# A two-layer streaming encoder on one core: the second queries' scores in two halves, side by side in the values' banks

## The chip, the cores and the metric

The kernel runs on one core of one Trainium2 chip. The engines that appear below are PE (TensorE, the matmuls, with its weight loads shown as PEld), DVE (VectorE), ACT (ScalarE), POOL (GpSimd) and SP (SyncE, which here only issues DMAs). The metric is the device time of one execution in microseconds. The three runs of the kernel before took 1877.65 to 1878.27 us, with a median of 1878.14 us.

## The reference: what is computed

One sequence of 256 positions and width 2048 goes through two layers. Cut to what matters here, a layer is:

```python
h = rmsnorm(x, norm_g)
proj = h @ w_in                       # 2048 x 11328, cut into nine parts
u = c_a * sigmoid(c_glu)
u = depthwise_causal_conv(u, width=31) + conv_b
y_conv = (silu(layernorm(u)) * silu(c_gate)) @ w_proj_conv
q  = rmsnorm(q_down) @ w_uq           # 16 heads, 128 plain + 64 rotary
kv = rmsnorm(kv_down) @ w_ukv         # 16 heads, 128 key + 128 value
s  = q . k / sqrt(192), masked by chunks of 64, in query blocks of 128
o  = softmax(s) @ v
y_mla = (o * silu(m_gate)) @ w_proj_mla
x = x + (sigmoid(g_conv) * y_conv + sigmoid(g_mla) * y_mla) @ w_out
```

All of it is in fp32.

## The kernel before

**Parts.** The matmuls take fp32r operands. To keep fp32 accuracy every operand is split in two, a high part (its value rounded to fp32r) and a low part (what is left), and three products are added: high by high, low by high, high by low. Weights arrive in pieces of two k-tiles (`raw`, 512 KB). ACT makes the high part (`split_hi`, L191: a copy, the rows `hi<-raw`), and DVE the low part (`split_lo`, L211: a subtraction, the rows `lo<-raw,hi`). The pool has four buffers for high parts (L195) and three for low parts (`split`, L140).

**Slots.** A block of a product has 512 columns (384 or 320 in a few), and for each piece of weights it issues twelve matmuls (`order_of_products`, L278): two query tiles, two k-tiles, three products. These twelve matmuls are a slot. `product` (L292) issues ahead of the matmuls of slot i the high parts of the pieces up to i+3 and the low parts up to i+2. After the matmuls it calls `background` (L243), where everything else of the slot is issued.

**The planner.** `at_slot` notes a step with the slot in which it is due and its estimated cost on DVE and ACT. `background` gives each engine a budget for the slot (the matmuls' time less its share of the splitting, L245-247), runs the steps that are due and books their costs, and then runs entries of the queue `fill` as long as the DVE budget is above zero (L256-260). An entry may also wait for a mark, and the entries of `apply` wait for ACT's budget too (`scalar`, L258). With what is left of ACT's budget `assist` makes taps of the convolution on ACT. At the end of the slot `finish_late` (L266) runs what was put in `late`. Engines execute in the order of issue: the class `InOrder` (L118) ties each instruction to the one before it.

**What is in `fill`.** The depthwise convolution: 31 taps for each of eight blocks of 256 channels (`conv`, L869), on DVE, either as two multiply-adds or as one addition of a tap that ACT has scaled. Behind them stands the LayerNorm (`layernorm`, L919): the sums over channels by two small matmuls (`mu`, `var`), the inverse root on DVE, `apply` (L987, DVE) with its `silu` on ACT a slot later (`soon`), the turned gates (`turned_gate`, DVE transposes), `gated` (L1109, DVE) and `separated` (L1117), which splits the result into the high and low parts of `ycT`, on ACT and DVE. Two of the sixteen channel tiles of `ycT` come from each block; four tiles are a group c, which `gated` and `separated` handle as one.

**Who needs it.** The product `pconv` multiplies with `ycT`. Its first block runs in eight slots, and group c is first used in the slots 2c and 2c+1. `before_pconv` (L1176) stands ahead of the matmuls of each of these slots: where group c has not been issued, it runs `fill` without regard to budgets until it has, and issues the parts.

**Attention.** The pairs of heads are staged twelve slots apart (`attention`, L681; due slots in L66-67). Scores are due 17 slots after the pair's `ukv` product, the exponentials at 19, the turned probabilities' split at 29, the values at 32, the outputs at 34. So the scores of a pair fall into the same slot as `split_p` of the pair before, and three slots ahead of that pair's values. `scores` (L750) writes the first 128 queries' scores into the PSUM tile `s0` with the keys' high and low parts in two halves, and the last 128 queries' scores (against 256 keys) into `s1`, five matmuls of 256 columns a head that accumulate in one place. `maxima` (L774) adds the halves of `s0`, masks, and takes the maxima on DVE; `exponentials` (L788) reads `s1` from PSUM. PSUM has eight banks: four for the products, two for the tile `tp` (the values' output `o_ps`, and `mu` and `var`), one each for `s0` and `s1`.

**In two other places** a low part is made close to its high part: `ukv_evac` (L666) puts the subtraction of the values' low part into `late` of the same slot, and `split_p` (L807) does so with the probabilities'. `scale_k` (L694) makes ACT's scaling of the keys and DVE's rotary part in turn, tile by tile. `glu_evac` (L853) puts the product of the gated unit (`product_out`) into `late`.

Of the kernel before, what the change touches and what calls it, by code (L numbers as in the profile page):

```python
# [15 lines left out]
ALU = mybir.AluOpType  # L16
# [98 lines left out]
def trunk(ctx: ExitStack, tc: tile.TileContext, xT, x, g_in, pos, win, wuq, wukv, wpc, wpm, wo, cst, rows, invf, out):  # L115
# [102 lines left out]

    steps, clock, late = [], [0], []
    fill, budget, marks, owed, assist = deque(), {"vec": 0.0, "act": 0.0}, {}, [], []

    def at_slot(ahead, f, vec=0.0, act=0.0, first=False):
# [18 lines left out]
    def background(n):  # L243
        clock[0] += 1
        slot = 12 * (n / 2400 + 0.0133) - 0.04  # L245
        for e, split_us in (("vec", KS * n / 960 + 0.06), ("act", KS * n / 1066 + 0.04)):
            budget[e] = min(budget[e], 0.0) + slot - split_us
        while True:
            due = [e for e in steps if e[0] <= clock[0]]
            if not due:  # L250
                break
            steps[:] = [e for e in steps if e[0] > clock[0]]
            for _, costs, f in due:
                spend(costs)
                f()
        while fill and budget["vec"] > 0:  # L256
            after, slots, scalar = fill[0][1]
            if after and clock[0] < marks.get(after, 1 << 30) + slots or scalar and budget["act"] < 0:  # L258
                break
            run_fill()  # L260

        while assist and budget["act"] > 0.8 and assist[0]():
            budget["act"] -= 0.85
        finish_late()
# [132 lines left out]
    def rms_factor(out_ap, sums, n):  # L397
        ms = small.tile(list(sums.shape), F32, tag=f"ms{sums.shape[-1]}", name="ms")
        vec.tensor_scalar(ms, sums, 1.0 / n, EPS, op0=ALU.mult, op1=ALU.add)
        rsqrt(out_ap, ms)  # L400


    zeros = work.tile([P, 256], F32R, tag="junk", name="zeros")
# [122 lines left out]
    for l in range(DEPTH):  # L526
# [24 lines left out]
            act.activation(down[:, t, at : at + n], ps, AF.Copy, scale=rinv_x[:, t : t + 1])  # L551

        def down_after(down=down, qkc=qkc, ss_d=ss_d, r_d=r_d, kpe=kpe, ccq=ccq, ssq_t=ssq_t, gqk=gqk, row=row, C=C, ss_base=ss_base):
            ka = work.tile([P, T, ROPE], F32, tag="qa", name="ka")
            kb = work.tile([P, T, ROPE], F32, tag="qb", name="kb")
            kp = down[:, :, 2 * LORA :]

            def squares(t):
# [95 lines left out]
        def rotate_q(b, pair_of=pair_of, ccq=ccq, ssq_t=ssq_t):  # L654
            p = pair_of(b)
            both = lambda a: a.rearrange("p t (a c) -> p (t a) c", a=2).unsqueeze(2).broadcast_to([P, 2 * T, 2, HALF])
            qa = work.tile([P, T, 2, 2, HALF], F32, tag="qa", name="qa")
            qb = work.tile([P, T, 2, 2, HALF], F32, tag="qb", name="qb")
            qr = p["qr"].rearrange("p t a h c -> p (t a) h c")
            vec.tensor_mul(qa.rearrange("p t a h c -> p (t a) h c"), qr, both(ccq))  # L660
            vec.tensor_mul(qb.rearrange("p t a h c -> p (t a) h c"), qr, both(ssq_t))
            out = p["qk"][:, :, :, 4, :].rearrange("p t (h a) c -> p t h a c", h=2)
            vec.tensor_sub(out[:, :, :, 0, :], qa[:, :, 0], qb[:, :, 1])
            vec.tensor_add(out[:, :, :, 1, :], qb[:, :, 0], qa[:, :, 1])

        def ukv_evac(b, t, ps, pair_of=pair_of):  # L666

            p = pair_of(b)
            k = ps[:, : 2 * NOPE].rearrange("p (j h c) -> p j h c", j=4, h=2)
            v = ps[:, 2 * NOPE :].rearrange("p (h d) -> p h d", h=2)  # L670
            act.copy(p["vh"][:, t], v)
            act.copy(p["qk"][:, t, :, 2:4, :], k)
            late.append(lambda: vec.tensor_sub(p["vl"][:, t], v, p["vh"][:, t].bitcast(F32)))
            for h in range(2):
                junk = work.tile([P, 512], F32, tag="junk", name="junk")
                act.activation(
                    junk[:, :NOPE].rearrange("p (j c) -> p j c", c=32), k[:, :, h, :],
                    AF.Square, accum_out=p["ss"][:, 1, t, h : h + 1],
                )

        def attention(b, pair_of=pair_of, ss_d=ss_d, kpe=kpe, ccq=ccq, ssq_t=ssq_t, gqk=gqk, A=A):  # L681
# [11 lines left out]

            def scale_k():  # L694
                for t in range(T):
                    rk = st["r"][:, 1, t, :]
                    for h in range(2):
                        k = qk[:, t, :, 2 + h, :]
                        act.activation(k, k, AF.Copy, scale=rk[:, h : h + 1])
                    vec.tensor_mul(  # L700
                        qk[:, t, :, 5, :].rearrange("p (h a) c -> p h a c", h=2),
                        kpe[:, t].rearrange("p (a c) -> p a c", a=2).unsqueeze(1).broadcast_to([P, 2, 2, HALF]),
                        rk.unsqueeze(2).unsqueeze(3).broadcast_to([P, 2, 2, HALF]),
                    )
                out("qk", rows)

# [42 lines left out]

            def scores():  # L750
                s0 = s_p.tile([P, 2, 2, P], F32, tag="s0", name="s0")
                s1 = s_p.tile([P, 2, SEQ], F32, tag="s1", name="s1")

                for h in range(2):
                    qs = slice(0, P)
                    pe.matmul(s0[:, h], rope_t[:, 0, h, qs], rope_k[:, :, h, qs], start=True, stop=False)
                    pe.matmul(s0[:, h, 0, :], nope_t[:, 1, h, qs], nope_t[:, 2, h, qs], start=False, stop=False)
                    pe.matmul(s0[:, h], nope_t[:, 0, h, qs], nope_t[:, 2:4, h, qs], start=False, stop=True)
                for h in range(2):
                    qs = slice(P, SEQ)  # L760
                    terms = [
                        (rope_t[:, 0, h, qs], rope_t[:, 1, h, :]),
                        (nope_t[:, 0, h, qs], nope_t[:, 2, h, :]),
                        (nope_t[:, 0, h, qs], nope_t[:, 3, h, :]),
                        (nope_t[:, 1, h, qs], nope_t[:, 2, h, :]),
                        (rope_t[:, 0, h, qs], rope_l[:, h, :]),
                    ]
                    for n, (qa, ka) in enumerate(terms):
                        pe.matmul(s1[:, h, :], qa, ka, start=n == 0, stop=n == len(terms) - 1)
                st["s"] = s0, s1  # L770

                late.append(maxima)

            def maxima():  # L774
                s0, s1 = st["s"]
                sx = work.tile([P, 2, P], F32, tag="sx", name="sx")
                act.copy(sx, s0[:, :, 1, :])
                vec.tensor_add(sx, s0[:, :, 0, :], sx)
                for s, nkeys in ((sx, P), (s1, SEQ)):

                    vec.memset(s[:CHUNK, :, nkeys - CHUNK :], MASKED)
                nb = small.tile([P, T, 2], F32, tag="nb", name="nb")
                vec.tensor_reduce(nb[:, 0], sx, axis=AX.X, op=ALU.max, negate=True)
                vec.tensor_reduce(nb[:, 1], s1, axis=AX.X, op=ALU.max, negate=True)
                vec.tensor_mul(nb, nb, st["rs"])
                st["s"], st["nb"] = (sx, s1), nb

            def exponentials():  # L788

# [17 lines left out]
            def split_p():  # L807
                z = st["pr"].rearrange("p (b i s) -> p i b s", i=6, s=32)
                hi, lo = (A.pt[:, i].rearrange("p h (x b s) -> p (h x) b s", x=3, s=32) for i in range(2))

                def parts():
                    act.copy(hi, z)
                    vec.tensor_sub(lo, z, hi.bitcast(F32))

                late.append(parts)

            def values():

# [3 lines left out]
                for h in range(2):  # L822
                    o = st["o"][:, h]
                    pe.matmul(o, v[0][:, 0, h, :], pt[:, :, h, :SEQ], start=True, stop=False)
                    pe.matmul(o[:, 0, :], v[1][:, 0, h, :], pt[:, 0, h, :SEQ], start=False, stop=False)
                    pe.matmul(o[:, :, P:], v[0][:, 1, h, :], pt[:, :, h, SEQ:], start=False, stop=False)
                    pe.matmul(o[:, 0, P:], v[1][:, 1, h, :], pt[:, 0, h, SEQ:], start=False, stop=True)

            def outputs():
                o = A.o_sb[:, 2 * b : 2 * b + 2, :]  # L830
# [7 lines left out]
            at_slot(QK_TURN_AT, blockwise, 1.85)  # L838
            at_slot(NOPE_AT, split_nope, 0.0, 1.8)
            at_slot(ROPE_AT, split_rope, 0.0, 2.5)  # L840
            at_slot(SCORES_AT, scores, 1.85, 0.35)
            at_slot(EXP_AT, exponentials, 0.0, 3.3)
            at_slot(P_BACK_AT, lambda: back_in("p"))
            at_slot(P_TURN_AT, turn_p, 0.9)
            at_slot(P_SPLIT_AT, split_p, 0.9, 0.8)
            at_slot(VALUES_AT, values)
            at_slot(O_AT, outputs, 0.62, 0.6)

# [4 lines left out]
        def glu_evac(b, t, ps, us=us):  # L853
# [10 lines left out]
                vec.scalar_tensor_tensor(u, ps[:, :256], r, sg, op0=ALU.mult, op1=ALU.mult)  # L864
                turn(u, 256, lambda z: conv(b) if t == T - 1 else None, us[b][:, :, at : at + P], (0.4, 0.0))

            late.append(product_out)

        def conv(b, us=us, vs=vs, s1=s1, C=C):  # L869
            scaled = {}  # L870
# [314 lines left out]
        for kind, i, pl in planned:  # L1185
# [25 lines left out]
                product(pl, of_down(0), lambda t, ps, i=i: uq_evac(i, t, ps), costs=(0.0, 2.3))  # L1211
                at_slot(EVAC_AT + 1, lambda i=i: rotate_q(i), 1.2)
            elif kind == "ukv":
                product(pl, of_down(4), lambda t, ps, i=i: ukv_evac(i, t, ps), costs=(0.75, 2.6))
                attention(i)
                if i == NPAIR - 1:
                    layernorm()
# [125 lines left out]
```

## Time and profile before

| | |
|---|---|
| median of three runs | 1878.14 us (1877.65 to 1878.27) |
| profiled execution, own time | 1877.59 us |
| its span in the trace | 1875.8 us |
| PE busy | 1870.9 us, 8665 matmuls |
| PEld (weight loads) busy | 1583.1 us |
| DVE busy | 1577.6 us, 2419 instructions |
| ACT busy | 1369.1 us, 2482 instructions |
| POOL busy | 484.5 us |
| granted TensorE clock, mean | 1.0 |
| HBM | 236 GB/s over the span |

Busy times are those of the profile's first part. A matmul's row lasts until its result is out, and the rows of matmuls overlap, so PE's busy time is no measure of how close it is to its peak; the pace is read from when they start. Groups of instructions are named out<-in by the program's tiles; "x16" is a count, and the time after an arrow in brackets is idle time of the engine before the group and what ended it. Nearly all instructions stand under one line (L126, a helper that records them), so rows are told apart by tiles.

### The profile page before, as it was taken

The numbers are of one execution on the slowest core, as the hardware profiler recorded it, in microseconds if no ns is written. First come the engines' busy times: TensorE is split into PE (matmuls) and PEld (weight loads), VectorE is DVE, ScalarE is ACT, GpSimd is POOL, SyncE is SP. The second block draws the span as 40 slices with busy tenths as digits, with TensorE's granted clock in tenths as the row PEclk, the third lists the DMA queues.
The fourth block names the chain that finished last, engine by engine and source line by source line (L and its number), as shares of the span: only waits on it lengthen the run. The fifth ranks groups of instructions, "written<-read, shape, count | busy, mean of one in ns | idle before, by whom it ended". The sixth has DMA issues, their size and how long they took to land.

```text
span 1875.8 us, 27389 instructions
## 1 busy us (share of the span) xinstructions
PE 1870.9 (100%) x8665; PEld 1583.1 (84%) x8665; DVE 1577.6 (84%) x2419; ACT 1369.1 (73%) x2482; POOL 484.5 (26%) x942
## 2 busy tenths in 40 slices
PE   9999999999999999999999999999999999999999
PEld 8988888888888888888899888888888888888887
DVE  6899988889999988766679898888999999785664
ACT  7678888888888866644557688888899888574442
POOL 1055555432200000122221555555322000001210
PEclk9999999999999999999999999999999999999999
DMA  9677878777755566578876787786777555556774
GB/s 322 228 255 253 279 243 281 254 248 235 245 197 192 198 206 222 209 236 282 285 235 216 248 275 256 255 283 240 255 235 243 197 191 203 207 206 222 238 251 164
DMA packets 140113, 445.06 MB, mean 237 GB/s; under 512 B 23808, under 2 KB 29440, under 8 KB 139968
## 3 DMA queue, kind: packets, MB, share of 16 engines
q1 hardware_dynamic: 106272, 359.89, 55.7%
q0 software_dynamic: 32832, 82.62, 13.5%
q8 instruction: 68, 1.11, 0.2%
q10 hardware_dynamic: 864, 0.80, 0.1%
q14 instruction: 77, 0.63, 0.1%
HBM read 399.18 MB, written 44.04 MB: 236 GB/s over the span
## 4 chain that ended last, share of the span: by engine, by line
PE 100%; DVE 0%; DVEq 0%; issue 0%
PE acc L126 97%; PE s L126 2%; PE o_ps L126 1%; PE warm L126 0%; PE var L126 0%; PE mu L126 0%; DVE xres L126 0%; DVEq L1339 0%; DVE zeros L126 0%
## 5 line engine op out<-in xcount | busy, mean ns | idle before, releaser
L126 ACT CAST hi<-raw 128x1024 fp32r<-128x1024 f32 (+3 forms) x690 | 700.5, 1020 | 400.4 <-PE acc L126 349.0
L126 DVE TENSOR_TENSOR lo<-raw,hi 128x1024 fp32r<-128x1024 f32 (+3 forms) x690 | 814.1, 1183 | 193.6 <-PE acc L126 144.3
L126 PE MATMUL acc<-hi,hT 128*128 128x512 f32 (+2 forms) x1728 | 419.7, 382 | 0.0
L126 PEld LDWEIGHTS acc<-hi,hT 128*128 128x128 f32 x1728 | 319.6, 188 | 59.2
L126 ACT ACTIVATE tap<-u_t,cst 128x256 f32<-128x256 f32 x602 | 260.2, 497 | 3.2 <-DVE v_t L126 3.2
L126 PE MATMUL acc<-hi,h_hi 128*128 128x512 f32 (+2 forms) x864 | 260.8, 383 | 0.0
L126 PE MATMUL acc<-hi,h_lo 128*128 128x512 f32 (+2 forms) x864 | 260.1, 382 | 0.0
L126 PE MATMUL acc<-lo,h_hi 128*128 128x512 f32 (+2 forms) x864 | 229.6, 382 | 0.0
L126 PE MATMUL acc<-lo,hT 128*128 128x512 f32 (+2 forms) x864 | 229.3, 382 | 0.0
L126 DVE TENSOR_TENSOR v_t<-v_t,tap 128x512 f32<-128x512 f32 x301 | 207.0, 688 | 10.9 <-DVE v_t L126 0.5
L126 POOL DMA_DIRECT2D turned<-turn_d x88 | 49.1, 558 | 545.1 <-DVE v_t L126 315.8
L126 PEld LDWEIGHTS acc<-hi,h_lo 128*128 128x128 f32 x864 | 161.2, 188 | 30.2
L126 PEld LDWEIGHTS acc<-lo,h_hi 128*128 128x128 f32 x864 | 160.6, 188 | 30.0
L126 PEld LDWEIGHTS acc<-lo,hT 128*128 128x128 f32 x864 | 160.6, 188 | 29.9
L126 PEld LDWEIGHTS acc<-hi,h_hi 128*128 128x128 f32 x864 | 160.2, 188 | 29.1 <-ACT hi L126 0.2
L126 POOL DMA_DIRECT2D turn_d<-gate x184 | 100.1, 551 | 324.0 <-DVE gate L126 177.5
L126 DVE SCALAR_TENSOR_TENSOR v_t<-u_t,cst,v_t 128x256 f32<-128x256 f32 x358 | 153.8, 480 | 2.1
L126 PE MATMUL acc<-hi,ycT 128*128 128x512 f32 x512 | 127.8, 389 | 0.0
L126 PE MATMUL acc<-hi,yT 128*128 128x512 f32 x512 | 127.8, 389 | 0.0
L126 PE MATMUL acc<-hi,oT 128*128 128x512 f32 x512 | 127.7, 389 | 0.0
L126 PE MATMUL acc<-hi,qkc 128*128 128x512 f32 (+1 forms) x512 | 119.2, 364 | 0.0
L126 PEld LDWEIGHTS acc<-hi,ycT 128*128 128x128 f32 x512 | 96.1, 188 | 20.0
(169 smaller groups left out, 2209.9 us busy)
## 6 DMA issues: line engine op xcount, KB each, us to landing
raw<-in_win SPq DMA_DIRECT2D x382, 512.0 KB, 4.3
raw<-in_wpm SPq DMA_DIRECT2D x64, 512.0 KB, 3.2
raw<-in_wpc SPq DMA_DIRECT2D x64, 512.0 KB, 4.3
raw<-in_wo SPq DMA_DIRECT2D x64, 512.0 KB, 5.0
raw<-in_wukv SPq DMA_DIRECT2D x32, 512.0 KB, 3.6
turned<-turn_d POOLq DMA_DIRECT2D x56, 256.0 KB, 4.7
raw<-in_win SPq DMA_DIRECT2D x32, 384.0 KB, 4.7
raw<-in_wuq SPq DMA_DIRECT2D x32, 384.0 KB, 3.2
```

The lines of the kernel that those rows point to most:

```text
L126: ins = getattr(self.engine, name)(*a, **k)
```

## The change

The scores of the last 128 queries are no longer accumulated in one place. Their tile `s1` is now a tile of the pool `tp` (two banks, shared in turn with `o_ps`, `mu` and `var`), with the keys' high and low parts in two halves, as `s0` has them. Three matmuls a head, of 512, 256 and 512 columns, take the place of five of 256. `maxima` copies the second half of each to SBUF with ACT, adds the first half with DVE, and masks and reduces in SBUF. The sum of the second queries shares a buffer (`qab`) with the rotary products, which are now one tile in place of two. The exponentials read SBUF.

Beside this, other places are put in another order. The values' low part and the probabilities' low part are subtracted a slot after the high part (`at_slot(1, ...)`), with costs of their own. `scale_k` leaves the keys' rotary part and the DMAs behind it to `late`. The product of the gated unit goes into a new list, `early`, which runs ahead of `fill`. In `values` the second and the fourth matmul of a head change places. The planner's cost of the scores goes from (1.85, 0.35) to (2.5, 0.85), and 0.75 on `ukv` and 0.9 on `split_p` become 0.36 twice and 0.85 on the deferred steps.

```diff
             for _, costs, f in due:
                 spend(costs)
                 f()
+            while early:
+                early.pop(0)()
...
-            late.append(lambda: vec.tensor_sub(p["vl"][:, t], v, p["vh"][:, t].bitcast(F32)))
+            at_slot(1, lambda: vec.tensor_sub(p["vl"][:, t], v, p["vh"][:, t].bitcast(F32)), 0.36)
...
             def scale_k():
                 for t in range(T):
-                    rk = st["r"][:, 1, t, :]
                     for h in range(2):
                         k = qk[:, t, :, 2 + h, :]
-                        act.activation(k, k, AF.Copy, scale=rk[:, h : h + 1])
+                        act.activation(k, k, AF.Copy, scale=st["r"][:, 1, t, h : h + 1])
+                late.append(scale_rotary)
+
+            def scale_rotary():
+                for t in range(T):
                     vec.tensor_mul(
...
-                s1 = s_p.tile([P, 2, SEQ], F32, tag="s1", name="s1")
+                s1 = tp_p.tile([P, 2, 2, SEQ], F32, tag="tp", name="s1")
...
-                    terms = [
-                        (rope_t[:, 0, h, qs], rope_t[:, 1, h, :]),
-                        (nope_t[:, 0, h, qs], nope_t[:, 2, h, :]),
-                        (nope_t[:, 0, h, qs], nope_t[:, 3, h, :]),
-                        (nope_t[:, 1, h, qs], nope_t[:, 2, h, :]),
-                        (rope_t[:, 0, h, qs], rope_l[:, h, :]),
-                    ]
-                    for n, (qa, ka) in enumerate(terms):
-                        pe.matmul(s1[:, h, :], qa, ka, start=n == 0, stop=n == len(terms) - 1)
+                    pe.matmul(s1[:, h], rope_t[:, 0, h, qs], rope_k[:, :, h, :], start=True, stop=False)
+                    pe.matmul(s1[:, h, 0, :], nope_t[:, 1, h, qs], nope_t[:, 2, h, :], start=False, stop=False)
+                    pe.matmul(s1[:, h], nope_t[:, 0, h, qs], nope_t[:, 2:4, h, :], start=False, stop=True)
...
             def maxima():
-                s0, s1 = st["s"]
-                sx = work.tile([P, 2, P], F32, tag="sx", name="sx")
-                act.copy(sx, s0[:, :, 1, :])
-                vec.tensor_add(sx, s0[:, :, 0, :], sx)
-                for s, nkeys in ((sx, P), (s1, SEQ)):
+                sums = []
+                for s, nkeys, tag in zip(st["s"], (P, SEQ), ("sx", "qab")):
+                    sums.append(work.tile([P, 2, nkeys], F32, tag=tag, name="sx"))
+                    act.copy(sums[-1], s[:, :, 1, :])
+                for s, sx in zip(st["s"], sums):
+                    vec.tensor_add(sx, s[:, :, 0, :], sx)
+                for s, nkeys in zip(sums, (P, SEQ)):
                     vec.memset(s[:CHUNK, :, nkeys - CHUNK :], MASKED)
...
-                def parts():
-                    act.copy(hi, z)
-                    vec.tensor_sub(lo, z, hi.bitcast(F32))
-
-                late.append(parts)
+                late.append(lambda: act.copy(hi, z))
+                at_slot(1, lambda: vec.tensor_sub(lo, z, hi.bitcast(F32)), 0.85)
...
-                    pe.matmul(o[:, 0, :], v[1][:, 0, h, :], pt[:, 0, h, :SEQ], start=False, stop=False)
+                    pe.matmul(o[:, 0, P:], v[1][:, 1, h, :], pt[:, 0, h, SEQ:], start=False, stop=False)
                     pe.matmul(o[:, :, P:], v[0][:, 1, h, :], pt[:, :, h, SEQ:], start=False, stop=False)
-                    pe.matmul(o[:, 0, P:], v[1][:, 1, h, :], pt[:, 0, h, SEQ:], start=False, stop=True)
+                    pe.matmul(o[:, 0, :], v[1][:, 0, h, :], pt[:, 0, h, :SEQ], start=False, stop=True)
...
-            at_slot(SCORES_AT, scores, 1.85, 0.35)
+            at_slot(SCORES_AT, scores, 2.5, 0.85)
...
-            at_slot(P_SPLIT_AT, split_p, 0.9, 0.8)
+            at_slot(P_SPLIT_AT, split_p, 0.0, 0.8)
...
-            late.append(product_out)
+            early.append(product_out)
...
-                product(pl, of_down(4), lambda t, ps, i=i: ukv_evac(i, t, ps), costs=(0.75, 2.6))
+                product(pl, of_down(4), lambda t, ps, i=i: ukv_evac(i, t, ps), costs=(0.0, 2.6))
```

More of the change, by code (lines that the diff above doesn't have):

```diff
@@ L216, in split_lo @@
         done[i] = highs[i], lo, k.stop
-    steps, clock, late = [], [0], []
+    steps, clock, late, early = [], [0], [], []
     fill, budget, marks, owed, assist = deque(), {"vec": 0.0, "act": 0.0}, {}, [], []
@@ L400, in rms_factor, with rotary_tile @@
         rsqrt(out_ap, ms)
+    def rotary_tile():
+        qab = work.tile([P, 2, T, 2, ROPE], F32, tag="qab", name="qab")
+        return qab[:, 0], qab[:, 1]
     zeros = work.tile([P, 256], F32R, tag="junk", name="zeros")
@@ L553, in down_after @@
         def down_after(down=down, qkc=qkc, ss_d=ss_d, r_d=r_d, kpe=kpe, ccq=ccq, ssq_t=ssq_t, gqk=gqk, row=row, C=C, ss_base=ss_base):
-            ka = work.tile([P, T, ROPE], F32, tag="qa", name="ka")
-            kb = work.tile([P, T, ROPE], F32, tag="qb", name="kb")
+            ka, kb = (a[:, :, 0, :] for a in rotary_tile())
             kp = down[:, :, 2 * LORA :]
@@ L656, in rotate_q @@
             both = lambda a: a.rearrange("p t (a c) -> p (t a) c", a=2).unsqueeze(2).broadcast_to([P, 2 * T, 2, HALF])
-            qa = work.tile([P, T, 2, 2, HALF], F32, tag="qa", name="qa")
-            qb = work.tile([P, T, 2, 2, HALF], F32, tag="qb", name="qb")
+            qa, qb = (a.rearrange("p t a (h c) -> p t a h c", h=2) for a in rotary_tile())
             qr = p["qr"].rearrange("p t a h c -> p (t a) h c")
@@ L702, in scale_k @@
                         kpe[:, t].rearrange("p (a c) -> p a c", a=2).unsqueeze(1).broadcast_to([P, 2, 2, HALF]),
-                        rk.unsqueeze(2).unsqueeze(3).broadcast_to([P, 2, 2, HALF]),
+                        st["r"][:, 1, t, :].unsqueeze(2).unsqueeze(3).broadcast_to([P, 2, 2, HALF]),
                     )
@@ L774, in maxima @@
             def maxima():
-                s0, s1 = st["s"]
-                sx = work.tile([P, 2, P], F32, tag="sx", name="sx")
-                act.copy(sx, s0[:, :, 1, :])
-                vec.tensor_add(sx, s0[:, :, 0, :], sx)
-                for s, nkeys in ((sx, P), (s1, SEQ)):
+                sums = []
[5 more added lines that the diff above has]
+                for s, nkeys in zip(sums, (P, SEQ)):
                     vec.memset(s[:CHUNK, :, nkeys - CHUNK :], MASKED)
                 nb = small.tile([P, T, 2], F32, tag="nb", name="nb")
-                vec.tensor_reduce(nb[:, 0], sx, axis=AX.X, op=ALU.max, negate=True)
-                vec.tensor_reduce(nb[:, 1], s1, axis=AX.X, op=ALU.max, negate=True)
+                for t in range(T):
+                    vec.tensor_reduce(nb[:, t], sums[t], axis=AX.X, op=ALU.max, negate=True)
                 vec.tensor_mul(nb, nb, st["rs"])
-                st["s"], st["nb"] = (sx, s1), nb
+                st["s"], st["nb"] = sums, nb
             def exponentials():
```

## The prediction

> **What bounds the kernel now.** I read the waits of PE first, then the chain that ended last, then the stretch of the timeline in which DVE and ACT hand work to PE with the least to spare. The waits of PE are one row, at the very start:
>
> ```profile
> PE warm L126 <- DVE zeros L126: 1.2, 1, 1.2
> ```
>
> So PE waits for nothing after its first matmul, and the time is the sum of its matmuls. The chain says the same, and gives their pace:
>
> ```profile
> 240.84 1.89 PE s L126 x16
> 242.73 8.19 PE acc L126 x36
> ...
> 285.40 1.11 PE o_ps L126 x8
> ```
>
> A matmul of 512 columns takes 8.19/36 = 227.5 ns; a pair's sixteen score matmuls (fourteen of 256 columns, two of 128) take 1.89 us, 118 ns each; its eight value matmuls 1.11 us. The span is 1875.8 us and the execution's own time 1877.59, 1.8 more, and 0.55 below the median of the runs.
>
> With PE never idle, a change has two ways to move the time: fewer or shorter matmuls, or a wait that is not there now. For the second I looked for where PE's operands arrive last. In the attention DVE and ACT are far ahead. The close place is the first layer's `pconv`, whose first block needs `ycT` group by group, two slots each:
>
> ```profile
> 764.62 1.98 PE L126 MATMUL acc<-hi,ycT 128*128 128x512 f32 x8
> ...
> 775.50 1.98 PE L126 MATMUL acc<-hi,ycT 128*128 128x512 f32 x8
> ...
> 780.94 1.98 PE L126 MATMUL acc<-hi,ycT 128*128 128x512 f32 x8
> ```
>
> These rows are the slots 280, 284 and 286 of the program, the first uses of groups 0, 2 and 3; a slot is (780.94-775.50)/2 = 2.72 us. The DVE rows that end in group 3:
>
> ```profile
> 769.79 1.22 DVE L126 TENSOR_TENSOR lo<-raw,hi 128x1024 fp32r<-128x1024 f32 x1
> 770.93 0.71 DVE L126 STREAM_TRANSPOSE turned<-turned 128x512 f32<-128x512 f32 x1
> 771.67 0.76 DVE L126 TENSOR_TENSOR v_t<-turned,v_t 128x256 f32<-128x256 f32 x2
> 772.35 0.71 DVE L126 STREAM_TRANSPOSE turned<-turned 128x512 f32<-128x512 f32 x1
> ...
> 775.88 1.29 DVE L126 TENSOR_TENSOR ycT<-v_t,ycT 128x512 fp32r<-128x512 f32 x2
> ...
> 781.20 1.23 DVE L126 TENSOR_TENSOR lo<-raw,hi 128x1024 fp32r<-128x1024 f32 x1 [1.50 <-PE acc L126]
> ```
>
> Group 3 is complete at 775.88+1.29 = 777.17 and first used at 780.94: 3.8 us to spare, less than two slots. The last row matters as much: DVE may not make a low part until PE has finished the slot whose buffer it takes. Slot 285 ends at 780.94, and the row starts 0.26 us later.
>
> **The change part by part.** *Matmuls.* Each pair drops four of sixteen score matmuls, and the columns stay 3840. With one price per matmul and one per column, 1.89 us for 16 and 3840 columns and 227.5 ns for one of 512 give 21.6 ns a matmul: 64 x 21.6 = 1.4 us less over sixteen pairs. If instead a narrow one keeps 118 ns and a wide one 227.5, four wide and two narrow take 1146 ns for ten times 118 = 1180, which is 0.55 us less in all. I take 1.0, between the two. The changed order in `values` keeps counts and columns (2304); by the two prices its eight would take 1.10 us and take 1.11, so at most 0.2 us is in it over sixteen pairs, of either sign: nothing.
>
> [...]
>
> *Added work.* The price of the addition and the copy is that of the same shapes at the values' output, and the cost of taps is that of the row below:
>
> ```profile
> L126 DVE TENSOR_TENSOR o_sb<-o_ps,o_sb 128x512 f32<-128x512 f32 x16 | 11.0, 685 | 0.2
> ...
> L126 DVE TENSOR_TENSOR v_t<-v_t,tap 128x512 f32<-128x512 f32 x301 | 207.0, 688 | 10.9 <-DVE v_t L126 0.5
> ...
> L126 DVE TENSOR_TENSOR pv<-pr,pv 128x768 fp32r<-128x768 f32 x16 | 15.3, 958 | 13.1 <-ACT pv L126 13.1
> ...
> L126 DVE TENSOR_TENSOR qk<-kpe,r_p 128x128 f32<-128x128 f32 x32 | 7.9, 288 | 13.7 <-POOL r_p L126 13.7
> ```
>
> ```profile
> L126 ACT COPY o_sb<-o_ps 128x512 f32<-128x512 f32 x16 | 9.4, 587 | 0.0
> ```
>
> DVE gets 16 x 0.685 = 11.0 us, ACT 16 x 0.587 = 9.4 us. On the other side the deferred low parts and the rotary part in `late` remove most of DVE's idle 13.1 and 13.7 us behind `pv` and `qk`. The scores' chain (copy, addition, reductions) ends some 0.7 us later in its slot, and the next use of its result is two slots (5.4 us) away: covered. In `tp`, `s1` is read out within its slot and the values come three slots (8.2 us) later: covered. The values' low part a slot later, and the gated unit's product earlier in its slot, change only when a product's PSUM bank comes free, and that bank is taken again two blocks later: covered.
>
> *Where it is not covered.* The fills are placed by the planner's costs, and not by when DVE is really idle; the idle time that goes does not bring them forward. A pair's booked DVE cost grows by 2.5-1.85 = 0.65 us less 0.08 of the deferred steps: 0.57 x 8 = 4.6 us a layer. ACT's grows too, and five taps fewer are made there. The build's order shows the effect exactly. Counting how many low parts DVE makes ahead of a step (slot i's matmuls have i+5 ahead of them):
>
> ```
>                                   before  after   last place in time
> layer 1, last sum of the conv        256    259
> first apply                          274    279
> parts of group 0 (slot 280)          278    282    285
> parts of group 1 (slot 282)          282    285    287
> parts of group 2 (slot 284)          285    289    289
> parts of group 3 (slot 286)          288    291    291
> layer 2, parts of group 3            624    628    635
> ```
>
> The tail is three slots late, and `apply` two more, because it also waits for ACT's budget behind `gconv`. Groups 2 and 3 now stand at the last possible place: `before_pconv` issues them itself, right ahead of the matmuls that read them. In front of them in DVE's queue is a low part that cannot start before the slot before has ended. So PE must stand still for the whole chain behind it, twice. In layer 2 there are seven places left (19 us): no wait.
>
> *First wait, slot 284.* The build has on ACT: a high part, the loading of the Silu table, four `silu`, the copies of group 2. On DVE: a low part, two multiplications, a transpose, two multiplications, the low parts. ACT's is the longer. Its rows:
>
> ```profile
> 736.71 1.06 ACT L126 CAST hi<-raw 128x1024 fp32r<-128x1024 f32 x1 [1.67 <-PE acc L126]
> 737.79 1.28 ACT L126 ACT_TABLE_LOAD   x1
> 739.08 1.10 ACT L126 ACTIVATE v_t<-v_t,cst 128x256 f32<-128x256 f32 x2
> ...
> 755.40 2.08 ACT L126 ACTIVATE v_t<-v_t,cst 128x256 f32<-128x256 f32 x4
> 757.38 1.04 ACT L126 CAST hi<-raw 128x1024 fp32r<-128x1024 f32 x1
> 758.33 1.13 ACT L126 CAST ycT<-v_t 128x512 fp32r<-128x512 f32 x2
> ...
> 780.23 1.05 ACT L126 CAST hi<-raw 128x1024 fp32r<-128x1024 f32 x1 [1.62 <-PE acc L126]
> ```
>
> The high part's buffer comes free 0.7 us ahead of a slot's end (780.23 against 780.94). From there: 1.08 (736.71 to 737.79), 1.29 for the table (to 739.08), 1.98 for four `silu` (755.40 to 757.38), 0.6 for the first copy: 4.95 us, so PE starts slot 284 4.3 us late. Its third matmul reads the low part, which DVE makes 0.69 us behind the copy, 0.45 us of which two matmuls cover: 0.25. Together 4.5 us. The bounds: 3.3 if the table is loaded earlier (1.28 less), 5.3 if DVE's queue, which has a transpose more ahead of the low part (0.7), turns out the longer.
>
> *Second wait, slot 286.* DVE's chain is the longer: 0.26, then 1.14 (769.79 to 770.93), 0.74 and 0.68 (to 772.35), 0.7 for the second transpose, 0.4 for the first of two multiplications, then ACT's copy 0.6: 4.5 us, and 0.25 as above: 4.8 us. The bounds: 4.0 if the first transpose (0.74) gets ahead, 5.5 if the copy waits for both multiplications (0.3 more) and none of the low part's 0.69 is covered.
>
> *Group 1, slot 282.* Its copies stand behind the last `gconv` sigmoids on ACT. Adding up the queue from the rows above they end within half a microsecond of the first use: 0 to 0.5 us, taken as 0.
>
> **Sum:** -1.0 + 4.5 + 4.8 = +8.3 us on 1877.6, 1885.9; against the median of the runs 0.55 more, 1886.5 us.
>
> **The rivals.** *Hidden after all (not slower).* One mechanism: the `pconv` tail has room for its delay. It decides at 3.8 us, what group 3 has to spare now, while the build puts it three places (8.2 us) later. What speaks for it: DVE loses some 27 us of idle waits, and could run the tail early. Against it: a low part waits for PE's slot, so no lead of DVE carries over. The time would be 1878.1-1.0 = 1877.1.
>
> *The matmul saving isn't there.* The columns are the same; at 0 instead of 1.0, with both waits, 1887.5. It lies within the range.
>
> *The clock falls in the waits.* The trace shows the slow pace at the start, after idleness:
>
> ```profile
> 1.19 4.00 PE L126 MATMUL warm<-zeros 128*128 128x256 f32 x17 [1.19 <-DVE zeros L126]
> ```
>
> Seventeen matmuls of 256 columns in 4.0 us are some 235 ns each, twice the scores' 118. If PE came out of one wait so, and stayed so for the same 4.0 us, it would lose 2.0 us: 1888.5, and 1890.5 for both. No row of this trace has PE idle for over 1.2 us and then working, so whether 4.5 us is enough isn't seen. [...]
>
> *DVE late in every pair.* The 0.685 us could reach PE in each pair: 16 x 0.685 = 11 us, with the two waits 1897. Against it:
>
> ```profile
> 244.80 2.08 DVE L126 TENSOR_TENSOR lo<-raw,hi 128x1024 fp32r<-128x1024 f32 x2
> ```
>
> After the scores at 240.84 to 242.73 DVE is back at low parts at 244.80, making those that PE takes from 248 on, so 0.7 us is there to spare.
>
> **How the numbers follow.** I count a difference of 0.2% (3.8 us) as what a measurement can tell. Both waits at full clock: 0.50, 1886.5, its own range by the bounds 1884.0 to 1888.4 (matmuls -1.4 to -0.5, waits 7.3 to 10.8). Both waits and one or two spells at the slower clock: 0.27, 1888.5 to 1890.5; the trace has the slow pace after idleness but no idle stretch of this length, so I give it about a third of the 0.77 in which both waits come. Hidden, or only one wait, below 1882: 0.14. Late in every pair, or more waits around `pconv`: 0.09. For 8 in 10 the range is 1883.5 to 1891. Faster by over 0.2% needs 3.8 us where the matmuls hold 1.4 at most: 0.02. Within 0.2%: 0.10. Slower: 0.88.
>
> **What would show it.** The waits of PE get rows of 4 to 5 us at `acc` on ACT's or DVE's `ycT`, two in layer 1 between 770 and 795 us and none in layer 2. The sixteen scores' stretches become twelve matmuls and some 0.05 us shorter, to 1.84 us. A granted clock under 1.0 behind 775 us would speak for the clock's rival, and waits at `acc` between 170 and 460 us for lateness in the pairs. A wait list that still has the one row at the start proves the forecast wrong.

## The result, and the profile after

The changed kernel took 1891.68 us (median of six runs, 1890.93 to 1892.3) against 1877.96 us of the kernel before (six runs, 1877.45 to 1878.33). The ratio is 1.0073 with a 95% interval of 1.0063 to 1.0083: 13.7 us slower. The forecast was 1886.5 us with a range up to 1891.0, so the sign was right and the size too small. The profiled execution took 1891.92 us with a span of 1890.1 us, 14.3 more than the span before.

The waits of PE in the changed kernel (engine, what waited and for whom; sum in us, times, longest):

```profile
PE acc L126 <- ACT ycT L126: 9.0, 2, 4.6
PE warm L126 <- DVE zeros L126: 1.2, 1, 1.2
```

There are two new waits, both for `ycT`, and no other. PE's timeline of the first layer shows where they stand (start, duration, tiles, count, and in brackets the idle time before):

```profile
774.60 1.07 PE L126 MATMUL acc<-lo,ycT 128*128 128x512 f32 x4
780.12 3.78 PE L126 MATMUL acc<-hi,ycT 128*128 128x512 f32 x8 [4.45 <-ACT ycT L126]
783.70 1.76 PE L126 MATMUL acc<-lo,ycT 128*128 128x512 f32 x4
785.29 2.00 PE L126 MATMUL acc<-hi,ycT 128*128 128x512 f32 x8
787.13 1.07 PE L126 MATMUL acc<-lo,ycT 128*128 128x512 f32 x4
792.78 3.78 PE L126 MATMUL acc<-hi,ycT 128*128 128x512 f32 x8 [4.58 <-ACT ycT L126]
...
801.14 1.98 PE L126 MATMUL acc<-hi,ycT 128*128 128x512 f32 x8
```

The rows at 780.12 and 792.78 are slots 284 and 286. Four matmuls take 0.91 us (782.75 to 783.66 below), so slot 284 was due at 774.60 + 0.91 = 775.51 and came 4.61 us late. Slot 286 was due at 787.13 + 0.91 = 788.04 and came 4.74 us late. But the eight matmuls behind each wait last 3.78 us, where they lasted 1.98 before. The time by stretches shows why. Behind the start and end of a stretch stand its length, the busy time of PE, PEld, DVE, ACT and POOL with counts, the granted TensorE clock (1.00 is full speed), the share of the DMA engines and what they moved in GB/s:

```profile
771.51:774.92 3.41, 3.41 (x17) 2.83 (x16) 2.52 (x4) 1.05 (x1) 0.00 (x0) 1.00 0.73 245
774.92:778.33 3.41, 0.75 (x4) 0.29 (x2) 3.41 (x6) 3.17 (x4) 0.00 (x0) 1.00 0.73 229
778.33:785.16 6.83, 5.04 (x12) 3.94 (x13) 2.22 (x5) 3.30 (x6) 0.00 (x0) 0.50 0.19 71
785.16:788.58 3.42, 3.04 (x14) 2.16 (x12) 1.51 (x2) 1.05 (x1) 0.00 (x0) 1.00 0.23 77
788.58:791.99 3.41, 0.00 (x0) 0.00 (x0) 3.34 (x7) 0.00 (x0) 0.00 (x0) 1.00 0.57 217
791.99:798.81 6.82, 6.03 (x14) 4.73 (x15) 2.17 (x5) 2.19 (x3) 0.00 (x0) 0.50 0.02 7
798.81:802.23 3.42, 3.42 (x16) 2.82 (x16) 1.55 (x2) 1.06 (x1) 0.00 (x0) 1.00 0.44 155
```

PE ran at half its clock for 6.83 us around the end of each wait. It was busy for 5.04 and 6.03 us of these and did half as much in them (from start to start, the eight matmuls at 780.12 took 783.70 - 780.12 = 3.58 us, where eight took 1.81 before), so about 5.5 us were lost.

The 14.3 us of the spans can be added up from rows. The four slots 284 to 287 begin in the kernel before at 775.50 (quoted in the prediction) and end with these rows of its timeline:

```profile
782.75 1.07 PE L126 MATMUL acc<-lo,ycT 128*128 128x512 f32 x4
783.66 1.52 PE L126 MATMUL acc<-hi,ycT 128*128 128x512 f32 x6
...
786.38 1.98 PE L126 MATMUL acc<-hi,ycT 128*128 128x512 f32 x8
```

They took 786.38 - 775.50 = 10.88 us before, and 801.14 - 775.51 = 25.63 after: 14.75 more. Of these 4.61 + 4.74 = 9.35 are the two waits, and the other 5.40 are the slower clock, with whatever of the low part's lateness is not hidden behind it. The first scores came 0.44 us later (172.85 and 173.29 below), and what is left, 14.3 - 14.75 - 0.44 = -0.9 us, is what the matmuls saved. The scores show 0.64 of that: they took 174.74 - 172.85 = 1.89 us before and 175.14 - 173.29 = 1.85 after, sixteen times. The first two rows are the kernel before, the second two the changed one:

```profile
172.85 2.05 PE L126 MATMUL s<-qk_t 128*128 128x256 f32 x16
174.74 0.63 PE L126 MATMUL acc<-hi,h_hi 128*128 128x512 f32 x2
```

```profile
173.29 2.01 PE L126 MATMUL s<-qk_t 128*128 128x256 f32 x12
175.14 0.63 PE L126 MATMUL acc<-hi,h_hi 128*128 128x512 f32 x2
```

### The profile page after: what moved, and what is told of

It reads as the page before. It is cut to its first block, busy times and chain, and to the rows that moved or that the text cites. A ratio compares the mean times of both kernels' runs of the same rounds, so it can differ in the third digit from the quotient of the medians.

```text
span 1890.1 us, 27256 instructions
## 1 busy us (share of the span) xinstructions
PE 1876.2 (99%) x8601; PEld 1583.9 (84%) x8601; DVE 1586.9 (84%) x2440; ACT 1373.4 (73%) x2488; POOL 484.6 (26%) x942
## 4 chain that ended last, share of the span: by engine, by line
PE 58%; DVE 0%; ACT 0%; DVEq 0%; issue 0%; ACTq 0%
PE acc L126 57%; PE s L126 1%; PE o_ps L126 0%; DVE turned L126 0%; DVE lo L126 0%; DVE v_t L126 0%; ACT ycT L126 0%; DVE xres L126 0%; DVEq L1339 0%; PE var L126 0%; PE mu L126 0%; DVEq L126 0%; ACTq L126 0%
## 5 line engine op out<-in xcount | busy, mean ns | idle before, releaser
L126 PE MATMUL acc<-hi,ycT 128*128 128x512 f32 x512 | 131.7, 398 | 9.0 <-ACT ycT L126 9.0
```

The source lines that it names most:

```text
L126: ins = getattr(self.engine, name)(*a, **k)
```

## The experiments

Three questions had to be told apart: whether the added work or its booked cost makes the waits, which booking does it and through which step, and what of the 13.7 us is the clock.

**The booking alone.** This is the kernel before with nothing but the scores' costs changed.

```diff
-            at_slot(SCORES_AT, scores, 1.85, 0.35)
+            at_slot(SCORES_AT, scores, 2.5, 0.85)
```

> The kernel before with one edit: the planner's cost of the scores is (2.5, 0.85) in place of (1.85, 0.35); no work is added and no instruction changes, only where the planner puts the fills. Theory of the place (what costs the time is that the first layer's groups 2 and 3 of the LayerNorm's tail are issued right ahead of the matmuls that read them): the built order has these groups at the same last places as the changed kernel (289 and 291), so PE waits twice for ACT's ycT, some 4.5 us each, and loses some 5.5 us to the slower clock behind the waits; without the 0.9 us that the matmuls save it takes 1877.96 + 14.6 = 1892.5 us. Rival, the work (DVE's 11.0 us and ACT's 9.4 us that are added make them late): none of this work is here, so 1878.0 us and no wait of PE.

It took 1891.77 us, ratio 1.0072 (1.0059 to 1.0085): the whole loss, with none of the new instructions.

```profile
PE acc L126 <- ACT ycT L126: 8.8, 2, 4.6
```

The wait at the start is the only other one.

**The change without its booking.** The changed kernel with the scores booked at (1.85, 0.35).

> The changed kernel with one edit: the planner's cost of the scores is (1.85, 0.35) again; all the added work stays. Theory of the place: the built order has groups 2 and 3 at 285 and 287, as in the kernel before or a place earlier, so PE does not wait at pconv, and the matmuls' saving shows: 1877.96 - 0.9 = 1877.1 us, the list of PE's waits has its one row at the start. Rival, the work: DVE and ACT do 11.0 and 9.4 us that the planner knows nothing of, so they come late for low parts in the attention or for the tail, with waits of PE of 5 to 11 us: 1882 to 1889 us.

It took 1877.48 us, ratio 0.9997 (0.9989 to 1.0006). All the added work is in it, and PE's only wait is the one at the start:

```profile
PE warm L126 <- DVE zeros L126: 1.2, 1, 1.2
```

So the addition and the copy in every pair cost PE nothing. The two kernels together settle the first question: the waits come from a number in the planner, not from DVE's or ACT's time.

**Each half of the change on the old bookings.** One kernel has the scores and maxima of the change with the old orders, the other the new orders with the old scores and the old order in `values`.

> The kernel before with the second queries' scores in halves in the values' banks (three matmuls a head, ACT's copy, DVE's addition, qab shared), and nothing else: the other orders and all bookings stay as before. Theory of the place: the tail's places are those of the kernel before, so no wait of PE at pconv; the scores' stretch is 0.04 us shorter a pair, 0.64 us over sixteen: 1877.3 us. Rival, the work: lateness of DVE or ACT in the pairs, over 1880 us. Rival, the orders (the deferred low parts and the rest are needed to hide the added work): PE waits in the attention by some 0.5 us a pair, 1886 us.

> The kernel before with the other orders alone (the values' and the probabilities' low parts a slot later, the keys' rotary part in late, the gated unit's product in early, with their costs), scores, their booking and the values' matmuls as before. Theory of the place: the tail is issued a place earlier than in the kernel before (277, 281, 285, 287), PE has nothing to wait for in either: 1878.0 us, no change within 0.3 us. Rival, the orders (they cost the time): PE waits in the list, and up to 14 us of the loss here, 1882 to 1892 us.

They took 1877.63 us (0.9997, 0.9988 to 1.0006) and 1877.67 us (0.9999, 0.999 to 1.0008). Neither can be told from the kernel before. The second has no wait but the one at the start, the first one more:

```profile
PE acc L126 <- ACT hi L126: 0.2, 1, 0.2
```

**Which booking, and through which step.** In the changed kernel only ACT's booking is taken back:

```diff
-            at_slot(SCORES_AT, scores, 2.5, 0.85)
+            at_slot(SCORES_AT, scores, 2.5, 0.35)
```

> The changed kernel with the scores booked at (2.5, 0.35): only the booked cost on DVE is raised, that on ACT stays at its old value. Theory, the DVE booking moves the tail: the build puts the parts of groups 0 to 3 at 282, 285, 289, 291 low parts, as in the changed kernel, so PE waits twice for ycT, 9.0 us by the list of waits (8.5 to 9.5), the clock falls in both, and the time is 1891.7 us (1890.5 to 1892.5). Rival, it is ACT's booking that holds apply and its silu back: without it both waits go, 1877.1 to 1880.

It took 1890.78 us, ratio 1.0068 (1.0051 to 1.0085), with 8.8 us of waits for `ycT`, so DVE's booking is enough. It differs from the changed kernel on its old bookings (1877.48 us) by that one number. ACT's booking raised alone was not run. In the other kernel all bookings stay and `apply` no longer waits for ACT's budget:

```diff
-                fill.append((lambda: f(*args), (after, slots, f is apply)))
+                fill.append((lambda: f(*args), (after, slots, False)))
```

> The changed kernel, bookings and all, with the condition taken out by which entries of apply wait for ACT's budget. The parts of groups 0 to 3 then stand at 281, 283, 287, 289 low parts, groups 2 and 3 two places earlier than in the changed kernel and one to two later than in the kernel before. Theory, it is the place in the queue that costs and nothing that DVE or ACT does in more time: the waits for ycT go or shrink to tenths, and the time is 1877.1 to 1879.7 us. Rival, DVE and ACT are truly late with this work, so the parts are issued earlier but done no earlier: PE still waits 7 us or more, 1886 to 1892 us.

It took 1877.61 us, ratio 0.9997 (0.9988 to 1.0007). No wait for `ycT` is left:

```profile
PE warm L126 <- DVE zeros L126: 1.2, 1, 1.2
PE acc L126 <- ACT hi L126: 0.7, 2, 0.5
```

The places in the build's order, counted as in the prediction (last place in time 285, 287, 289, 291 for the four groups):

```
                          group 0   1    2    3    median, us
kernel before                 278  282  285  288   1877.96
changed kernel                282  285  289  291   1891.68
booking alone                 282  285  289  291   1891.77
only DVE's booking            282  285  289  291   1890.78
changed, old bookings         277  281  285  287   1877.48
scores alone, old orders      278  282  285  288   1877.63
new orders alone              277  281  285  287   1877.67
apply without ACT's budget    281  283  287  289   1877.61
parts issued one earlier      282  285  288  290   1886.28
parts issued two earlier      282  285  287  289   1879.65
```

The last two rows are kernels of the last experiment below. Every kernel of the table with groups 2 and 3 at the last place loses 12.7 us or more. The delay is made in two steps: DVE's booking makes the convolution's tail late, and `apply`, late already, then waits for ACT's budget. Without this condition on `apply` the booking costs nothing.

The place of a group's last step does not say everything. The kernels with 287 and 289 have groups 2 and 3 at the same places, and the one in which only the parts are issued earlier took 2.0 us more. Its list of waits has 1.1 us for `ycT`, and its low parts come late. DVE's rows for group 3, first with the parts issued two earlier, then with `apply` free of ACT's budget:

```profile
779.50 0.70 DVE L126 STREAM_TRANSPOSE turned<-turned 128x512 f32<-128x512 f32 x1
...
782.82 1.29 DVE L126 TENSOR_TENSOR ycT<-v_t,ycT 128x512 fp32r<-128x512 f32 x2 [0.40 <-ACT ycT L126]
```

```profile
779.40 1.29 DVE L126 TENSOR_TENSOR ycT<-v_t,ycT 128x512 fp32r<-128x512 f32 x2
```

In the first kernel the group's two transposes and its multiplications still stand right in front of its low parts, which start 3.4 us later than in the second.

**What the clock costs.** In the changed kernel PE is kept busy in the waits with n matmuls on data that lies ready:

```diff
+            if l == 0 and j in (4, 6):
+                busy = tp_p.tile([P, 512], F32, tag="tp", name="busy")
+                for n in range(20):
+                    pe.matmul(busy, h_hi[:, 0, :P], h_hi[:, 0:2, :].rearrange("p a s -> p (a s)"), start=n == 0, stop=n == 19)
```

> The changed kernel, with twenty matmuls of 512 columns whose result nobody reads put ahead of the slots 284 and 286 of the first layer, into a free tile of tp. They take 20 x 0.227 = 4.5 us, the time for which PE waits there. If the clock falls because PE is idle: the groups arrive no earlier, but PE's clock stays, and the 5.5 to 5.9 us lost at the slower pace go: 1891.7 - 5.7 = 1886.0 us, granted clock 1.0, PE's waits for ycT under 0.5 us. Rival (the slow matmuls are something else, such as reading operands just written): no gain, 1891 to 1892 us.

> As with twenty, but eight matmuls (1.8 us): PE is still idle for 2.7 to 2.8 us twice. If the clock falls only for idleness that fills most of a window of 3.4 us, it may fall in one of them or in none: 1886.0 us without, 1888.9 with one spell. If any idleness of 2.7 us is enough: 1891.7 us as without the matmuls.

Of the window of 3.4 us in the expectation with 8 matmuls the changed kernel's trace shows a spacing: its clock changes at 778.33, 785.16, 791.99 and 798.81 us, 6.82 or 6.83 us apart, twice 3.41. With 20 it took 1887.41 us, ratio 1.0049 (1.0034 to 1.0064), with 8 it took 1890.5 us, ratio 1.0065 (1.0048 to 1.0082). With 20 the granted clock was 1.0 throughout, and slot 284 began where it begins in the changed kernel, at 780.14:

```profile
775.52 4.70 PE L126 MATMUL busy<-h_hi 128*128 128x512 f32 x20
780.14 2.38 PE L126 MATMUL acc<-hi,ycT 128*128 128x512 f32 x8
782.36 1.07 PE L126 MATMUL acc<-lo,ycT 128*128 128x512 f32 x4
```

So useless matmuls made the kernel 1891.68 - 1887.41 = 4.3 us faster. That is the net price of the slower clock: at full clock the low part's lateness shows, 782.36 - 780.14 = 2.22 us for eight matmuls that take 1.81 (780.94 to 782.75 before), 0.4 us that half the clock hides: there the eight took 3.58 us, no more than twice 1.81. Twice 0.4 us make up most of the difference to the 5.40 us above.

**How much idleness brings the clock down.** With 8 the waits were 5.4 us in all, 2.8 the longest, and the clock still fell in both. Four more kernels shorten the idleness, two with 12 and 16 such matmuls, two by having the parts issued one or two pieces earlier:

```diff
-            c = j * KS // 4
+            c = min(j + 1, 7) * KS // 4     # the second kernel: j + 2
```

> The changed kernel with before_pconv issuing each group one slot ahead of its first use (bookings stay). The built order has groups 2 and 3 at 288 and 290. The chains then start 2.72 us earlier, so PE should wait 4.5 - 2.7 = 1.8 us each: with idleness that short the clock should hold: 1877.1 + 3.6 to 4.0 = 1880.9 us. If the clock falls all the same: 1886 us. Rival, the work: about 1891 us as before, since the places are not the cause.

> The changed kernel with before_pconv issuing each group two slots ahead of its first use (bookings stay): places 287 and 289. The chains of 4.95 and 4.75 us have 5.4 us, so no wait of PE is left or only tenths: 1877.1 us, up to 1878.0. Rival, the work: about 1891 us.

> The changed kernel with 12 matmuls of 512 columns, whose result is not read, ahead of slots 284 and 286 of the first layer; they take some 2.8 us of each wait, so about 1.8 us of idleness is left in each (8 of them left 2.8 us and the clock fell in both). If an idleness of 1.8 us is enough wherever it falls, the clock falls in both again, PE's mean granted clock is 0.998 or less and the time 1890 us. If it depends on where the idleness lies in the gate's windows, the clock falls in one or none: 1887.4 (none, as with 20) to 1889.

> As with 12, with 16 such matmuls (3.7 us), so that about 0.9 us of idleness is left in each wait. An idleness of 0.75 us left the clock at 1.0 where the parts were issued two pieces earlier: if the threshold lies above 0.9 us the granted clock stays at 1.0 and the time is 1887.4 us as with 20; if it lies below, 1889 to 1890 us.

One piece earlier took 1886.28 us, ratio 1.0043 (1.0028 to 1.0058), with waits of 3.06 and 1.82 us, where 1.8 was expected for each, and the clock fell in both. That it would hold through 1.8 us was the author's estimate. Two pieces earlier took 1879.65 us, ratio 1.0007 (0.9998 to 1.0017), with waits of 0.34 and 0.75 us at a clock of 1.0. At most 1878.0 had been expected. Beside the waits, the eight matmuls behind each took some 0.4 us more than 1.81, as with the 20 matmuls above. With 12 and 16 matmuls single runs gave 1887.81 and 1887.8 us, both at a clock of 1.0. So a wait of 1.82 us cost the clock in one kernel, and one of 1.86 us did not in another:

```profile
787.99 2.79 PE L126 MATMUL acc<-hi,ycT 128*128 128x512 f32 x8 [1.82 <-ACT ycT L126]
```

```profile
791.18 2.38 PE L126 MATMUL acc<-hi,ycT 128*128 128x512 f32 x8 [1.86 <-ACT ycT L126]
```

The first row is of the kernel one piece ahead, the second of that with 12 matmuls. Length alone does not decide. The trace records when the clock changes, and in all these kernels the changes lie whole multiples of 3.41 us apart (one piece ahead at 779.53, 782.94, 789.77 and 793.18 us). This spacing is all that the traces record of the windows in the expectation with 12 matmuls. With 12 matmuls no change lies near the waits, so there the cuts are counted on in steps of 3.41 us from its change at 4.67 us. Cut at these times, the time by stretches of the kernel one piece ahead reads:

```profile
776.12:779.53 3.41, 0.99 (x3) 0.57 (x4) 2.97 (x7) 2.33 (x5) 0.00 (x0) 1.00 0.29 117
779.53:782.94 3.41, 3.41 (x9) 2.64 (x9) 1.42 (x2) 1.30 (x2) 0.00 (x0) 0.50 0.30 66
...
786.35:789.77 3.42, 1.78 (x7) 1.18 (x8) 2.98 (x6) 2.09 (x3) 0.00 (x0) 1.00 0.27 105
789.77:793.18 3.41, 3.41 (x10) 2.63 (x9) 1.23 (x2) 1.04 (x1) 0.00 (x0) 0.50 0.48 142
```

and that of the kernel with 12 matmuls:

```profile
776.09:779.50 3.41, 2.76 (x13) 1.95 (x11) 3.38 (x7) 3.38 (x6) 0.00 (x0) 1.00 0.74 220
779.50:782.91 3.41, 2.32 (x9) 1.63 (x10) 1.54 (x3) 1.56 (x4) 0.00 (x0) 1.00 0.29 113
...
786.33:789.74 3.41, 3.00 (x14) 2.14 (x12) 3.00 (x5) 0.50 (x1) 0.00 (x0) 1.00 0.60 193
789.74:793.15 3.41, 1.97 (x7) 1.34 (x8) 2.28 (x5) 1.14 (x2) 0.00 (x0) 1.00 0.27 107
```

Compare PE's busy time in a stretch with the clock of the next. Behind 0.99 and 1.78 us of work the next stretch ran at half. Behind 1.97 us and more it ran at full clock. In the second kernel both waits fell across a boundary, and neither stretch lost enough. From these two kernels the boundary would lie between 1.78 and 1.97 of 3.41 us. The first wait of the kernel with the booking alone does not fit that:

```profile
774.34:777.75 3.41, 1.52 (x7) 0.94 (x5) 3.41 (x7) 2.69 (x3) 0.00 (x0) 1.00 0.76 269
777.75:781.17 3.42, 1.13 (x4) 0.66 (x5) 2.84 (x6) 2.76 (x6) 0.00 (x0) 1.00 0.47 159
781.17:784.58 3.41, 3.41 (x10) 2.63 (x9) 0.14 (x1) 1.05 (x1) 0.00 (x0) 0.50 0.00 0
```

Here 1.52 us of work left the next stretch at full clock, and only the 1.13 us of that next one brought it down. The rows agree again if the stretches that count end some 0.2 us ahead of the recorded change. The three nearest to the boundary are then these, of the kernel one piece ahead (the clock fell), of the booking alone and of that with 12 matmuls (it stayed):

```profile
786.15:789.57 3.42, 1.60 (x7) 1.02 (x7) 2.98 (x6) 2.09 (x3) 0.00 (x0) 1.00 0.32 125
```

```profile
774.14:777.55 3.41, 1.72 (x8) 1.10 (x6) 3.41 (x6) 2.49 (x3) 0.00 (x0) 1.00 0.76 270
```

```profile
789.54:792.95 3.41, 1.77 (x7) 1.16 (x7) 2.48 (x5) 1.14 (x2) 0.00 (x0) 1.00 0.33 119
```

So by an estimate from these rows the boundary lies between 1.60 and 1.72 of 3.41 us, about half. The 0.2 us is fitted to them afterwards, and no run tested it.

## Why the prediction fell short

**What bounds the kernel** (PE never idle, only new waits count): right. Where the waits went away the time was back at 1877.5 to 1877.7.

**Matmuls, -1.0:** about -0.9 by the remainder of the spans; the scores' stretch is 1.85, forecast as 1.84. The medians cannot show so little: the change on its old bookings came out at 0.9997 (0.9989 to 1.0006). *The values' order, nothing:* the 0.9 less the scores' 0.64 leaves some 0.2 us to it, a gain, at the edge of the bounds given. The spans behind the first scores agree: 1876.4 - 174.09 = 1702.3 us with the scores alone, and 1875.3 - 173.24 = 1702.1 with the whole change on its old bookings.

**Added work, covered:** right, shown by the change on its old bookings, which has only the wait at the start.

**The booked costs put the tail late:** right, and the whole cause of the waits. The prediction named DVE's cost and ACT's budget behind `apply`. The kernel with only DVE's booking and the one with `apply` free of ACT's budget bear out both.

**First wait, 4.3 us (4.5 with the low part):** 4.61. **Second wait, 4.5 (4.8):** 4.74. ACT's chain ahead of slot 284 in the changed kernel:

```profile
775.12 1.05 ACT L126 CAST hi<-raw 128x1024 fp32r<-128x1024 f32 x1 [1.99 <-DVE v_t L126]
776.19 1.28 ACT L126 ACT_TABLE_LOAD   x1
777.48 2.07 ACT L126 ACTIVATE v_t<-v_t,cst 128x256 f32<-128x256 f32 x4
779.46 1.12 ACT L126 CAST ycT<-v_t 128x512 fp32r<-128x512 f32 x2
```

From the high part at 775.12 to PE's start at 780.12 it is 5.0 us, forecast as 4.95. It began 0.4 us ahead of the slot instead of 0.7, because DVE's `v_t` held it back. Two such waits and none in layer 2 were forecast, and so it was. *Group 1, nothing:* no wait there.

**The step that failed** is the first of "how the numbers follow": both waits at full clock, with 0.50, against 0.27 for the rival in which the clock falls. The sum has no term for the clock. The clock fell in both waits, and that term measured 5.40 us. Without it the forecast's sum holds to 0.9 us: with 20 matmuls in the waits the kernel took 1887.41, and the forecast was 1886.5. Its other terms measured 0.1 to 0.3 us more each. The rival was the right account and its size was off too: for 1890.5 it charged 2.0 us a wait, as PE was slow for 4.0 us at the start of the kernel. The slow stretches lasted 6.83 us each and cost 5.4 us together. PE was still waiting when each began, and a first half in which it worked only in part, for 1.62 and 2.62 of 3.41 us, did not bring the clock back.

The 0.27 is about a third of the 0.77, and that third was the author's estimate: no run shows such a share. In the three kernels that waited twice for 4.2 to 4.6 us (changed, booking alone, only DVE's booking) the clock fell in all six waits. The stretch of 3.41 us ahead of the changed kernel's second fall had no work at all (788.58 to 791.99), but in the stretch ahead of the first PE still worked for 0.75 us, and in the kernel one piece ahead one with 1.78 us of work was enough.

**The other rivals.** Hidden after all: it gave 1877.1, and is nearly what happened (1877.61) where `apply` did not wait for ACT's budget, though not in the changed kernel. The missing matmul saving and lateness in every pair did not happen.

## What to carry to other kernels

Where a planner places work by booked costs, a raised cost can delay the work behind it even if the engine has time to spare, so compare places in the order of issue, of the whole chain and not only of its last step, with the last places at which PE can still get its operands. Two parts of such a chain may each be harmless and together cost a stall. Two cures worked here: to book as before, and to let the tail go without one of the conditions. Price a stall of PE with the clock that it loses: here 9.35 us of waits cost 14.75.

## What the runs showed of the hardware

The granted clock fell after far shorter idleness than expected: a wait of 1.82 us was enough where it left PE only 1.78 us of work in a 3.41 us stretch ahead of the recorded change, while waits of 1.74 and 1.86 us across the boundary of two stretches left it at 1.0. At half clock the stretches with 1.62 and 2.62 us of PE work were followed by another at half, and one with 3.02 us by full clock; these are the first halves of the two slow stretches of the changed kernel, and the second slow stretch of that with 8 matmuls:

```profile
778.33:781.74 3.41, 1.62 (x4) 1.29 (x5) 2.22 (x5) 2.26 (x5) 0.00 (x0) 0.50 0.38 143
...
791.99:795.40 3.41, 2.62 (x6) 2.10 (x7) 1.66 (x4) 1.14 (x2) 0.00 (x0) 0.50 0.03 13
```

```profile
792.17:795.58 3.41, 3.02 (x7) 2.40 (x8) 1.29 (x2) 0.86 (x2) 0.00 (x0) 0.50 0.02 7
```

That the share of work in a stretch is what decides, and that the stretch ends some 0.2 us ahead of the recorded change, is read from these few waits. No run varied either alone.
